# Buffers of raw weights in the MLPs of a two-layer diffusion block: two pools in turn, or each pool by the number of its buffers

## The chip, the cores and the metric

The kernel runs as one program on one core of one Trainium2 chip. The metric is device time in microseconds, as the median of several runs. One further run is recorded by the hardware profiler, and the profile's numbers come from that one. Engines are named as the profile names them: PE is TensorE's matmuls and PEld its weight loads, DVE is VectorE, ACT is ScalarE, POOL is GpSimd. SP is the engine that issues most transfers; its queue is worked off in order.

## The reference

The block has a latent stream of 256 tokens and a context of 256 tokens, with 2048 channels in float32. Two layers follow each other. The first mixes tokens with a bidirectional RWKV-7 recurrence, the second with a gated long convolution (Hyena). After each mixer comes a dense MLP with a squared ReLU, 2048 to 8192 channels and back. Each part stands between two RMS norms, with shift, scale and gate computed from a conditioning vector (adaLN):

```
h = modulate(rms_norm(x, norm_g[i, 2]), mod[:, 3], mod[:, 4])
x = x + mod[:, 5] * rms_norm(squared_relu_mlp(h, mlp_up[i], mlp_down[i]), norm_g[i, 3])
```

Here `squared_relu_mlp(h, w_up, w_down)` is `square(relu(h @ w_up)) @ w_down`, and `mod` is `silu(c) @ ada_w[i] + ada_b[i]`, a product of one row with a matrix of 2048 by 12288 per layer. The weights of one MLP take 128 MB in float32, and each is used once.

## The kernel before

**Products in three terms.** A float32 operand is split into a high part, which ScalarE rounds to the format that TensorE multiplies, and a low part, the rest, which VectorE subtracts (`split_into`). `mm3` then multiplies high by high, high by low and low by high into one accumulator in PSUM. All large products are made so.

**Weights.** `load_split` (L139) brings one block of weights: it takes a raw tile `w` of 128 by 2048 float32 (1 MB), issues its transfer on SP, and splits it in halves of 1024 columns into tiles `wh` and `wl`, the cast on ScalarE and the subtraction on VectorE. A raw tile is free again when its last half has been split. A split half is free when the last matmul that reads it has been done.

**Pools.** `open_weights` (L86) opens a pool of raw tiles (`wraw`) and a pool of split halves (`wsp`) and puts each into a list. From layer 0's output projection to the end one pair is open, with two raw tiles and three halves of each part. Inside `mlp` (L1489) a second pair is opened beside it, `MLPW = (1, 3)`: one raw tile and three halves. So an MLP has three raw tiles and six halves; the products around it have two and three. `turn` (L94) moves the last pool of a list to its front and takes the tile from it. With one pool in the list it always gives that pool; within a pool the tiles go round.

**The MLP.** `mlp` runs in four parts of 2048 hidden channels. Each part first makes the up product (`gemm_ws`, L176): the weights stand in TensorE, and 258 columns stream through (256 tokens and two columns for the shift). A load of 1 MB gives 48 such matmuls. Eight blocks of 256 channels take two loads each. The first part begins with a lead (`lead`): its first two blocks are made side by side from eight loads of 512 KB, so that the first matmuls need only the first channels of the normalised input `hx`, which `resid` (L433) of the part before makes one block of channels after the other. The results are evacuated to `nt`, squared, and split into `uh` and `ul`. Then the down product (`gemm_tok`, L211) adds 16 loads of 1 MB into eight accumulators, two at a time, with 24 matmuls of 512 columns to a load. There are 132 loads in an MLP.

**Beside it.** During the MLPs a generator, `ada_run` (L304), computes the adaLN rows that later layers need. It loads tiles `aw` of 512 KB on the same SP queue (two buffers) and accumulates them into `acc`, on VectorE for the rows computed in the first MLP, on ScalarE and GpSimd for later ones. `tick` advances it after each weight load, at a rate that spreads it over the MLP.

**Order.** The order of the instructions on each engine is made once, when the program is built: a planner goes through the instructions by priority (mostly program order), gives out tiles of the pools, and when an instruction has to wait for a tile, a later one of the same queue can be placed ahead of it. On the chip each engine works its list in order.

Of the kernel before, what the change touches and what calls it, by code (L numbers as in the profile page):

```python
# [69 lines left out]
class Kern:  # L70
# [15 lines left out]
    def open_weights(self, es, raw=2, sp=3):  # L86

        for l, n, b in ((self.wraw, "wraw", raw), (self.wsp, "wsp", sp)):
            if b:
                l.append(self.pool(es, n, b))  # L90
                es.callback(l.pop)

    @staticmethod
    def turn(pools):  # L94
# [1792 lines left out]
```

## Time and profile before

| what | value |
|---|---|
| runs | 3564.54, 3571.8 and 3573.12 us, median 3571.8 us |
| the profiled execution's own time | 3562.79 us |
| its span | 3561.0 us |
| granted TensorE clock, mean | 0.974 |
| PE busy | 3312.7 us, 93% of the span |
| DVE, ACT, POOL busy | 2450.2, 1738.5 and 435.3 us |
| moved from and to HBM | 777.31 MB read, 54.59 MB written |
| first MLP, issues of its weights after the product before it | 1456.8 to 2227.0 us |
| second MLP, the same | 2772.1 to 3512.6 us |

The span runs from the first to the last instruction of the program. A group of instructions is given with its source line; most operations of the two engines ACT and DVE go through one helper (L53) and all large matmuls through another (L111), so the groups are told apart by the names of the tiles: `wh<-w` is a cast of raw weights, `wl<-w,wh` a subtraction, `mm<-wh,uh` a matmul of the down product, `mm<-hxh,wh` one of the up product, `acc<-aw,sc,acc` a step of the adaLN rows. "Idle before" is the time that an engine stood still just before an instruction, with what ended it. The chain of waits follows the work that ended last back to what released it.

### The profile page before, as it was taken

How to read it: one execution, taken by the hardware profiler on the slowest of the kernel's cores; microseconds unless marked ns; L12 is line 12 of the kernel's file. 1: busy time of each engine (PE TensorE's matmuls, PEld its weight loads, DVE VectorE, ACT ScalarE, POOL GpSimd, SP SyncE). 2: the span in 40 equal slices, each digit the busy share in tenths (PEclk: the TensorE clock that was granted, in tenths of full speed). 3: DMA queues.
4: the chain of work that ended last, by engine and by line, in shares of the span. 5: the costliest groups of instructions: out<-in, count | busy, mean ns of one | idle time of the engine just before them, and what ended most of it. 6: DMA issues, size and time to landing. Idle time of an engine off the chain costs nothing.

```text
span 3561.0 us, 74541 instructions
## 1 busy us (share of the span) xinstructions
PE 3312.7 (93%) x30598; PEld 2890.3 (81%) x30598; DVE 2450.2 (69%) x3867; ACT 1738.5 (49%) x3070; POOL 435.3 (12%) x496
## 2 busy tenths in 40 slices
PE   6798888999999798999999999999999899999999
PEld 3476677878888666898979898898887798989897
DVE  4788776767777765687777776688786675555554
ACT  4554454545544454443434345566564664434343
POOL 0011121111111000000000002134441530000000
PEclk9999999999999899999999999999999999999999
DMA  9668898999988646678888887566665775565563
GB/s 309 208 221 291 270 344 265 286 277 274 274 273 272 195 131 209 206 255 288 266 287 267 291 256 242 166 222 220 218 213 189 235 240 186 188 185 182 189 187 122
DMA packets 587808, 836.79 MB, mean 235 GB/s; under 512 B 39552, under 2 KB 373281, under 8 KB 587465
## 3 DMA queue, kind: packets, MB, share of 16 engines
q1 hardware_dynamic: 556360, 718.76, 62.9%
q0 software_dynamic: 31104, 113.26, 10.0%
q8 instruction: 239, 3.92, 0.4%
q14 instruction: 105, 0.85, 0.1%
HBM read 777.31 MB, written 54.59 MB: 234 GB/s over the span
## 4 chain that ended last, share of the span: by engine, by line
PE 54%; DMA 19%; DVE 14%; ACT 6%; issue 5%; POOL 2%; SPq 0%; ACTq 0%; DVEq 0%; POOLq 0%
PE mm L111 39%; DMA aw<-in_ada_w 10%; PE fl L111 5%; PE sg L111 5%; PE sc L111 4%; DVE wl L53 3%; POOL acc L329 2%; DVE acc L53 1%; DVE tmp L53 1%; DVE d L53 1%; ACT aw L53 1%; ACT wh L53 1%; DMA w<-in_mlp_down 1%; DVE xt L53 1%; DMA cum<-cum 1%
## 5 line engine op out<-in xcount | busy, mean ns | idle before, releaser
L53 DVE TENSOR_TENSOR wl<-w,wh 128x1024 fp32r<-128x1024 f32 (+1 forms) x716 | 912.5, 1280 | 514.6 <-ACT wh L53 511.2
L53 ACT CAST wh<-w 128x1024 fp32r<-128x1024 f32 (+1 forms) x716 | 737.8, 1043 | 694.0 <-PE mm L111 390.3
L111 PE MATMUL mm<-hxh,wh 128*128 128x258 f32 x2816 | 803.4, 286 | 13.0 <-DVE nt L53 11.6
L111 PE MATMUL mm<-hxh,wl 128*128 128x258 f32 x2816 | 801.4, 285 | 4.6 <-DVE wl L53 4.5
L111 PE MATMUL mm<-hxl,wh 128*128 128x258 f32 x2816 | 799.3, 284 | 0.0
L111 PEld LDWEIGHTS mm<-hxh,wh 128*128 128x128 f32 x2816 | 534.1, 190 | 16.9 <-DVE nt L53 9.0
L111 PEld LDWEIGHTS mm<-hxh,wl 128*128 128x128 f32 x2816 | 534.2, 190 | 8.2 <-DVE wl L53 6.8
L111 PEld LDWEIGHTS mm<-hxl,wh 128*128 128x128 f32 x2816 | 536.7, 191 | 1.8
L329 POOL TENSOR_TENSOR acc<-acc,aw 128x512 f32<-128x512 f32 x180 | 274.6, 1526 | 1341.4 <-ACT aw L53 1239.9
L111 PE MATMUL mm<-wh,uh 128*128 128x512 f32 x1024 | 405.5, 396 | 0.7 <-DVE nt L53 0.7
L111 PE MATMUL mm<-wl,uh 128*128 128x512 f32 x1024 | 400.7, 391 | 1.9 <-DVE wl L53 1.8
L111 PE MATMUL mm<-wh,ul 128*128 128x512 f32 x1024 | 402.4, 393 | 0.0
L53 DVE SCALAR_TENSOR_TENSOR acc<-aw,sc,acc 128x512 f32<-128x512 f32 x300 | 225.0, 750 | 102.7 <-DMA aw<-in_ada_w 100.5
L111 PEld LDWEIGHTS mm<-wl,uh 128*128 128x128 f32 x1024 | 192.4, 188 | 48.6 <-DVE wl L53 5.7
L111 PEld LDWEIGHTS mm<-wh,ul 128*128 128x128 f32 x1024 | 192.2, 188 | 45.6
L111 PE MATMUL fl<-fh,fx 128*128 128x256 f32 x1024 | 214.8, 297 | 13.2 <-DMA fx<-xv 11.2
L111 PEld LDWEIGHTS mm<-wh,uh 128*128 128x128 f32 x1024 | 192.3, 188 | 41.9 <-DVE nt L53 1.1
L111 PEld LDWEIGHTS fl<-fh,fx 128*128 128x128 f32 x1024 | 168.7, 194 | 31.5 <-DMA fx<-xv 14.6
L53 ACT ACTIVATE aw<-aw,sc 128x512 f32<-128x512 f32 x180 | 125.8, 719 | 131.0 <-DMA aw<-in_ada_w 128.0
L111 PE MATMUL fl<-flo,fx 128*128 128x256 f32 x512 | 146.0, 285 | 0.0
L111 PE MATMUL sg<-ard,KB 64*64 64x64 f32 (+1 forms) x3584 | 128.6, 244 | 13.9 <-ACT yf L53 4.5
L111 PEld LDWEIGHTS sg<-ard,KB 64*64 64x64 f32 x3584 | 110.0, 136 | 20.1 <-ACT yf L53 4.7
(361 smaller groups left out, 5867.5 us busy)
## 6 DMA issues: line engine op xcount, KB each, us to landing
aw<-in_ada_w SPq DMA_DIRECT2D x288, 512.0 KB, 6.0
w<-in_mlp_down SPq DMA_DIRECT2D x128, 1024.0 KB, 5.4
w<-in_mlp_up SPq DMA_DIRECT2D x120, 1024.0 KB, 6.6
fx<-xv POOLq DMA_DIRECT2D x128, 512.0 KB, 6.1
aw<-in_ada_w SPq DMA_DIRECT2D x192, 256.0 KB, 3.8
w<-in_hy_in_w SPq DMA_DIRECT2D x44, 1024.0 KB, 5.3
fx<-xr POOLq DMA_DIRECT2D x64, 512.0 KB, 5.7
w<-in_w_k SPq DMA_DIRECT2D x16, 1024.0 KB, 7.5
```

What stands on the lines that cost most here:

```text
L53: return self.kern.pin(self.key, f(*a, **kw))
L111: return self.pin("pe", self.nc.tensor.matmul(out, lhsT=lhsT, rhs=rhs, **kw))
L329: nc.gpsimd.tensor_tensor(acc, acc, w[:, a], op=ALU.add)
```

## The change

The list of pools gets each pool as often as the pool has buffers, where it had each pool once. `turn` is unchanged and still moves the last entry to the front. When the pools of an MLP are closed, every entry of that pool is taken out of the list, where before the last entry was popped.

```
         for l, n, b in ((self.wraw, "wraw", raw), (self.wsp, "wsp", sp)):
             if b:
-                l.append(self.pool(es, n, b))
-                es.callback(l.pop)
+                p = self.pool(es, n, b)
+                l.extend([p] * b)
+                es.callback(lambda l=l, p=p: l.__setitem__(slice(None), [q for q in l if q is not p]))
```

In an MLP the list of raw tiles was outer, own and is now outer, outer, own. From its start the raw tiles were taken own, outer, own, outer, and are now taken own, outer, outer, own, outer, outer. The list of split halves was outer, own and is now three times outer and three times own; halves were taken from the two pools in turn and are now taken three from the own pool, then three from the outer. Outside the MLPs a list holds one pool only, once or several times, and the tiles are taken as before. The number and size of the buffers, the loads and all computation are the same.

## The prediction

> **What bounds the kernel now.** I read the page first, then the busy times of stretches inside the two MLPs, then in the worst stretch the matmul groups, the chain of waits and the tile of raw weights.
>
> ```profile
> PE 3312.7 (93%) x30598; PEld 2890.3 (81%) x30598; DVE 2450.2 (69%) x3867; ACT 1738.5 (49%) x3070; POOL 435.3 (12%) x496
> GB/s 309 208 221 291 270 344 265 286 277 274 274 273 272 195 131 209 206 255 288 266 287 267 291 256 242 166 222 220 218 213 189 235 240 186 188 185 182 189 187 122
> w<-in_mlp_up SPq DMA_DIRECT2D x16, 512.0 KB, 5.3
> ```
>
> TensorE is busy 93% of the span. The change can give back only time in which TensorE stands in an MLP because raw weights are late. So I count matmuls. The columns are stretch, length, then busy time and count for PE, PEld, DVE, ACT and POOL, granted clock, DMA share and GB/s.
>
> ```profile
> 1530.00:1770.00 240.00, 240.00 (x1649) 223.61 (x1648) 183.97 (x260) 102.85 (x155) 0.00 (x0) 1.00 0.84 273
> 1770.00:1920.00 150.00, 143.64 (x824) 123.99 (x823) 110.86 (x145) 54.45 (x73) 0.00 (x0) 1.00 0.85 281
> ...
> 2070.00:2120.00 50.00, 47.83 (x392) 46.91 (x391) 35.75 (x52) 20.56 (x33) 0.00 (x0) 1.00 0.82 260
> ...
> 2900.00:3530.00 630.00, 630.00 (x3878) 566.57 (x3878) 350.27 (x418) 282.69 (x395) 2.31 (x2) 1.00 0.58 185
> 3100.00:3160.00 60.00, 60.00 (x262) 48.83 (x261) 29.61 (x29) 23.09 (x22) 0.00 (x0) 1.00 0.59 191
> 3020.00:3080.00 60.00, 60.00 (x501) 60.00 (x500) 36.20 (x51) 30.06 (x51) 0.00 (x0) 1.00 0.58 183
> ```
>
> The last two rows are pure stretches of the second MLP: a matmul of the down product takes 60/262 = 0.229 us, one of the up product 60/501 = 0.120 us. One load of 1 MB feeds 24 of the first or 48 of the second, so TensorE uses one up in 5.50 or 5.75 us.
>
> ```profile
> L111 PE MATMUL mm<-wl,uh 128*128 128x512 f32 x128 | 50.8, 397 | 1.9 <-DVE wl L53 1.8
> L111 PE MATMUL mm<-hxh,wh 128*128 128x258 f32 x136 | 39.0, 287 | 3.7 <-DVE nt L53 3.7
> L312 PE MATMUL sg<-ones,acc 128*128 128x2 f32 x32 | 3.8, 241 | 0.0
> ```
>
> Each product has three matmul groups of the same count, so 1770 to 1920 us holds 384 down, 408 up and 32 small ones (0.12 us each, like an up one): 87.9 + 48.9 + 3.8 = 140.6 us of work in 150, **9.4 us lost**. From 2070 to 2120 the 392 matmuls, nearly all up, need 47.0 of 50: **3.0 us lost**. From 1530 to 1770 and from 2900 to 3530 TensorE is never idle. So 12.4 us is what the steady parts can return, all in the first MLP.
>
> Who makes it wait, in 1770 to 1920 us, by the chain of waits and by the tile of raw weights:
>
> ```profile
> by line: DMA w<-in_mlp_down 20.2%; DMA aw<-in_ada_w 15.4%; DVE wl L53 15.3%; PE mm L111 13.3%; DVE acc L53 11.6%; DMA w<-in_mlp_up 9.2%; issue 7.3%; ACT wh L53 4.2%; DVE o L53 2.0%; DVE nt L53 0.7%; PE sg L312 0.5%; DVE mod L53 0.1%; ACTq L
> ...
> 1778.93 7.99 DMA w<-in_mlp_down
> 1786.99 1.06 ACT wh L53
> ...
> 1792.12 7.83 DMA w<-in_mlp_down
> ```
> ```profile
> L53 DVE TENSOR_TENSOR wl<-w,wh x49: 1212/1217/1225, 1770.2 to 1916.8; 128x1024 fp32r<-128x1024 f32 x49
> L53 ACT CAST wh<-w x49: 1027/1046/1054, 1770.7 to 1919.6; 128x1024 fp32r<-128x1024 f32 x49
> L53 SPq DMA_DIRECT2D w<-in_mlp_down x14: 367/368/368, 1771.4 to 1849.4; - x14
> L53 SPq DMA_DIRECT2D w<-in_mlp_up x11: 367/368/368, 1855.4 to 1918.0; - x11
> its engine sat idle before it (us, times) until:
>   DMA w<-in_mlp_down: 38.4, 7
>   DMA w<-in_mlp_up: 33.7, 5
> ...
> DMA to landing us min/median/max: 7.2/7.6/8.1
> ```
>
> The chain is a ring: a load is issued at 1778.93, lands 7.99 us later, its cast starts within 0.1 us, two casts and two subtractions follow, and the subtraction's end lets the next load go at 1792.12. A turn takes 13.19 us. ScalarE waits 72.1 us for 12 of these 25 loads: every second one is late.
>
> **The change part by part.** In the code before, load n of an MLP takes its slot by parity. Even loads share the one slot of the MLP's own pool, so load n waits for the split of load n−2; odd ones have the outer pool's two slots and wait for n−4. The ring above is the single slot's: one turn per two loads, 13.19/2 = 6.6 us per load, against the 5.50 us that TensorE needs. After the change the list holds the outer pool twice and the own pool once, so every load waits for the split of n−3: one turn per three loads, 13.19/3 = **4.4 us per load**, below 5.50. The k-th load on SP still goes when a third-last split ends, now in program order, so bytes and queue places stay nearly as they are. Nothing is added: the same loads, casts and subtractions.
>
> *Split halves.* The six halves before came one from each pool in turn; now three from one, then three from the other. Either way a half comes back after six: 0 us. The order would matter only with unequal pools.
>
> *The steady gain.* The raw-weight ring goes. The other ring in this stretch, the adaLN weights, stays:
>
> ```profile
> L53 DVE SCALAR_TENSOR_TENSOR acc<-aw,sc,acc x57: 739/747/754, 1773.4 to 1915.8; 128x512 f32<-128x512 f32 x57
> L53 SPq DMA_DIRECT2D aw<-in_ada_w x31: 367/368/368, 1770.0 to 1916.5; - x31
> ...
> DMA to landing us min/median/max: 3.8/5.3/7.5
> ```
> ```profile
> by line: PE mm L111 44.0%; DMA aw<-in_ada_w 13.4%; DMA w<-in_mlp_up 11.7%; DVE wl L53 11.0%; DVE acc L53 6.7%; issue 5.8%; DVE nt L53 2.2%; ACT wh L53 2.1%; PE sg L312 1.6%; DVE o L53 1.4%; DVE mod L53 0.1%; ACTq L53 0.1%; DVEq L53 0.1%
> ```
>
> Its turn is 0.37 + 5.3 + 2 × 0.75 = 7.2 us over two buffers, 3.6 us per load; with 31 of them beside 25 weight loads that is 4.5 us per 5.50, but at the longest landing (7.5 us) 5.8, which is too slow. So it is late only at times. By the chain's shares the weights' part of the loss is 29.4/44.8 of 9.4 us, 6.2, and (second row, 2070 to 2120) 11.7/25.1 of 3.0 us, 1.4: together 7.6. That leaves 4.8 us in which the adaLN load was last. Part of that is late only because VectorE and SP, both in order, stood behind a late split. Bounds: 0 (that ring takes the place at once) and 12.4. I take 7.6 plus half of 4.8, **−10.0 us**.
>
> *Second MLP, steady (2900 to 3530 us).* Nothing: the casts wait for TensorE, and loads land sooner.
>
> ```profile
>   PE mm L111: 284.2, 185
> ...
> DMA to landing us min/median/max: 5.0/5.3/7.4
> ```
>
> *The entries.* The MLP's own slot is also what lets its first loads run ahead while the product before is still working:
>
> ```profile
> 1372.31 0.59 SPq L53 DMA_DIRECT2D w<-in_mlp_up  x1
> ...
> 1380.76 0.37 SPq L53 DMA_DIRECT2D w<-in_mlp_up  x1
> ...
> 1386.82 0.69 SPq L53 DMA_DIRECT2D w<-in_mlp_up  x1
> ...
> 1399.73 0.37 SPq L53 DMA_DIRECT2D w<-in_mlp_up  x1
> ```
> ```profile
> 1390.00:1410.00 20.00, 17.70 (x77) 14.04 (x76) 8.56 (x9) 8.20 (x8) 0.00 (x0) 1.00 0.87 291
> ...
> 2820.00:2900.00 80.00, 76.68 (x622) 75.74 (x621) 59.45 (x67) 54.06 (x96) 44.67 (x29) 0.99 0.76 241
> ```
> TensorE's waits, from 1457 to 2290 us and from 2737 to 3561:
> ```profile
> PE mm L111 <- DVE nt L53: 10.0, 6, 4.1
> PE sg L459 <- DVE dg L53: 7.6, 2, 4.2
> ```
> ```profile
> PE sg L459 <- DVE dg L53: 12.2, 2, 9.6
> PE mm L111 <- DVE nt L53: 2.4, 2, 2.1
> ```
>
> The four issues ahead of the first MLP are its loads 0, 2, 4 and 6 of 512 KB, each issued when the slot's last split ended. After the change the slot holds loads 0 and 3, and load 3's split needs a half of the outer pool, so it stands until the earlier product lets one go. Two early loads and two early splits per entry move behind the product. In the first entry they leave a crowded moment (0 to 1.8 us of gain, 512 KB at 291 GB/s) and find gaps later, since TensorE then waits for the norm anyway (`dg`): 0. In the second entry ScalarE is busy 54 of 80 us with adaLN weights too: 0 to 2 × (1.05 + 1.22) = 4.5 us. The longest wait for the norm there, 9.6 us, covers most; I take a quarter, **+1.1**. After an MLP the outer pool's halves come free up to two halves later; without the same wait for `dg` at the MLP's end that would cost a half's matmuls, 2.8 us, with it 0.
>
> The sum is −10.0 + 1.1 = **−8.9 us**. The profiled execution took 3562.79 us (span 3561.0), so its like would take 3553.9. It is 9.0 us below the median of the runs, 3571.8, and near the fastest, 3564.54. On the median's footing the forecast is **3562.9 us**.
>
> **The rivals.**
>
> *The adaLN ring takes over.* If its loads are always the last, the weights come early for nothing: 0 to −3, time about 3570. For it: its landing of up to 7.5 us, and 15.4% of the chain. Against it: 4.5 us per load at the median. The Trainium skill, DMA: Bandwidth & Descriptors, section Issuing engines are not separate DMA queues, says that all DMAs run on the same 16 engines and interleave, by which a weight load sent earlier could only delay an adaLN load and the gain would be nil; but the number of loads in flight rises little, and the stretch moves 281 GB/s where one slice of the page moves 344, so the trace leaves it room.
>
> *More goes than the steady loss.* TensorE also waits early in each MLP for the up product's evacuation (`nt`, longest 4.1 us and 2.4 in all). If ScalarE, freed of its waits, serves these sooner, the whole 12.4 goes and 4.1 + 2.4 with it: −18.9, time 3552.9. Against it: the rows name VectorE, whose work the change leaves as it is.
>
> *Slower: the lost head start.* In the lead part TensorE consumes eight small loads. If loads 4 and 5, and then 7 and 8, each have to wait for a turn of the outer slots (0.37 + 5.3 landing + 1.05 + 1.22 = 7.9 us), each entry loses 15.9 us and both 31.8; less 10.0 that is +21.8, time **3593.6**. It decides once the two entries lose over 10 us together. For it: in the entry to the second MLP both DMA and ScalarE are loaded. Against it: the lead part is paced by the residual's columns, which come one after another, and loads 1 and 2 now have free halves waiting.
>
> *It does not do what it says.* Were the slots given out without regard to the turn, nothing would change. The pairing seen above (every second load late) speaks against that; it is in the first rival's time.
>
> **How the numbers follow.** Forecast 0.50, adaLN ring or no effect 0.18, more than the steady loss 0.20, slower 0.12. A measurement of this kernel can tell about 0.3% (10.7 us) from no change. Faster by more: all of the third case and 0.18 of the forecast's, 0.38. Slower: 0.11 of the last. Same: 0.51. The range reaches from the larger gain (3552.9, less 3 for runs as fast as the fastest) to 3575, the adaLN case with the highest run's 1.3 us and some of the entry cost; it leaves out most of the slower case.
>
> **What would show it.** Right: in the first MLP ScalarE's wait for raw weights falls from 72.1 us in the like of 1770 to 1920 to under 20; in the chain the weights' share falls below that of the adaLN load; TensorE's busy time there is near full; and ahead of the MLPs SP shows two small loads instead of four. Wrong: those waits stay; or they go while VectorE's wait for adaLN weights rises by as much; or TensorE idles in the lead parts.

## The result and the profile after

The changed kernel took **3555.46 us** (median of 8 runs, 3544.67 to 3563.14) beside 3573.61 us for the kernel before (8 runs, 3564.54 to 3580.38). The ratio is 0.9937, with a 95% interval of 0.9921 to 0.9954: 0.63% faster. The forecast was 8.9 us less than before; the medians differ by 18.2 us. Direction and main mechanism were right; the forecast had half of the size.

The two profiled executions show less than that. Here is the head of the page after:

```profile
span 3558.3 us, 74568 instructions
...
PE 3310.4 (93%) x30598; PEld 2894.7 (81%) x30598; DVE 2453.0 (69%) x3867; ACT 1749.9 (49%) x3070; POOL 436.7 (12%) x496
```

The span fell from 3561.0 to 3558.3 us, 2.7 us. So the spans can't be compared as they stand. Up to the output projection of layer 0 the two programs have the same instructions on every engine, yet that part took 1375.4 us in the profile before and 1389.6 us in this one; over all the profiles of this case it took 1370 to 1400 us. The table cuts that scatter off. Its stages are read from TensorE's instructions: from the first matmul of the output projection to the first down matmul of the first MLP ("entry 1"), from there to the last down matmul of that MLP ("MLP 1"), to the first down matmul of the second MLP ("entry 2", with the residual and Hyena), and to the last down matmul ("MLP 2"). An end of some 18 us follows. "Before, again" and "after, again" are one more profiled execution of each.

| kernel (us) | entry 1 | MLP 1 | entry 2 | MLP 2 | sum |
|---|---|---|---|---|---|
| before | 217.0 | 657.1 | 660.7 | 632.9 | 2167.7 |
| before, again | 218.7 | 658.5 | 662.3 | 632.9 | 2172.4 |
| after | 219.7 | 641.0 | 661.5 | 629.4 | 2151.6 |
| after, again | 220.4 | 641.0 | 659.5 | 629.4 | 2150.3 |

From the means, MLP 1 gives 16.8 us, MLP 2 gives 3.5, entry 1 costs 2.2 and entry 2 gives 1.0: 19.1 us, about what the runs show. Within a stage of an MLP the same kernel repeats to 1.4 us or better; an entry repeats to about 2 us, so what the entries cost or give is hardly told from nothing.

**Where the time went in MLP 1.** The busy time of the same stretches as before, after the change (stretch, length, PE, PEld, DVE, ACT, POOL, granted clock, DMA share, GB/s):

```profile
1770.00:1920.00 150.00, 150.00 (x907) 134.27 (x906) 117.82 (x157) 63.73 (x84) 0.00 (x0) 1.00 0.87 292
1920.00:2070.00 150.00, 150.00 (x906) 134.25 (x906) 119.28 (x163) 64.90 (x88) 0.00 (x0) 1.00 0.88 293
2070.00:2120.00 50.00, 50.00 (x421) 50.00 (x419) 41.94 (x63) 24.96 (x41) 0.00 (x0) 1.00 0.87 273
```

TensorE, which worked 143.64 of the first 150 us and 47.83 of the last 50, now works all of them. The chain of waits by line, for 1770 to 1920 us and for 2070 to 2120 us:

```profile
by line: PE mm L112 98.0%; PE sg L313 2.1%
...
by line: PE mm L112 97.1%; PE sg L313 3.1%
```

No transfer is left in it: neither the raw weights (29.4% before in the first stretch) nor the adaLN weights (15.4%). The tile of raw weights in 1770 to 1920 us (line numbers after are one higher):

```profile
L53 ACT CAST wh<-w x53: 1032/1049/1057, 1769.9 to 1919.0; 128x1024 fp32r<-128x1024 f32 x53
L53 DVE TENSOR_TENSOR wl<-w,wh x51: 1214/1218/1228, 1771.3 to 1918.5; 128x1024 fp32r<-128x1024 f32 x51
L53 SPq DMA_DIRECT2D w<-in_mlp_down x15: 367/368/368, 1772.6 to 1853.0; - x15
L53 SPq DMA_DIRECT2D w<-in_mlp_up x11: 367/368/368, 1859.1 to 1919.8; - x11
its engine sat idle before it (us, times) until:
  PE mm L112: 60.1, 36
...
DMA to landing us min/median/max: 5.8/6.7/7.4
```

ScalarE's 72.1 us of waits for raw weights are gone from this stretch. It waits 60.1 us for TensorE instead, that is, for a split half to come free: the weights now run ahead of the matmuls. Over the whole MLP, 1500 to 2250 us, the waits (us in total, times, longest) were before

```profile
ACT wh L53 <- DMA w<-in_mlp_down: 113.1, 23, 11.3
ACT wh L53 <- DMA w<-in_mlp_up: 111.4, 23, 11.2
...
ACT wh L53 <- PE mm L111: 48.4, 30, 4.5
...
DVE acc L53 <- DMA aw<-in_ada_w: 78.9, 44, 5.0
```

and are after

```profile
ACT wh L53 <- PE mm L112: 228.6, 151, 4.0
...
DVE acc L53 <- DMA aw<-in_ada_w: 78.5, 50, 3.7
...
ACT wh L53 <- DMA w<-in_mlp_down: 5.9, 3, 2.3
```

46 late loads of weights became 3. VectorE's wait for adaLN weights stayed what it was.

**MLP 2.** There was no stall to remove there, and still it is 3.5 us shorter. The rows that answer to those shown of before:

```profile
2900.00:3530.00 630.00, 629.51 (x3901) 568.26 (x3900) 352.78 (x423) 284.24 (x397) 2.72 (x2) 1.00 0.58 186
...
3100.00:3160.00 60.00, 60.00 (x264) 49.20 (x263) 30.10 (x29) 23.10 (x22) 0.00 (x0) 1.00 0.56 189
```

TensorE is full in both kernels but for 0.5 us, and in 60 us it makes 264 matmuls where it made 262. The distance from the start of one down matmul to the start of the next, the spacing, went from 230.7 to 229.0 ns in this MLP; over its 1536 down matmuls that is 2.7 us. That of its 2304 up matmuls went from 120.3 to 119.9 ns, 0.9 us. The prediction had no term for either.

### The profile page after: what moved, and what is told of

It reads as the page before. It is cut to its first block, busy times and chain, and to the rows that moved or that the text cites. A ratio compares the mean times of both kernels' runs of the same rounds, so it can differ in the third digit from the quotient of the medians.

```text
span 3558.3 us, 74568 instructions
## 1 busy us (share of the span) xinstructions
PE 3310.4 (93%) x30598; PEld 2894.7 (81%) x30598; DVE 2453.0 (69%) x3867; ACT 1749.9 (49%) x3070; POOL 436.7 (12%) x496
## 4 chain that ended last, share of the span: by engine, by line
PE 60%; DMA 16%; DVE 11%; ACT 5%; issue 4%; POOL 2%; SPq 1%; ACTq 0%; DVEq 0%; POOLq 0%
PE mm L112 45%; DMA aw<-in_ada_w 9%; PE sg L112 5%; PE fl L112 5%; PE sc L112 4%; POOL acc L330 2%; DVE tmp L53 1%; DVE wl L53 1%; DVE d L53 1%; ACT aw L53 1%; ACT wh L53 1%; DMA win<-in_window 1%; PE sc L414 1%; DMA cum<-cum 1%; PE sg L460 1%
## 5 line engine op out<-in xcount | busy, mean ns | idle before, releaser
L53 ACT CAST wh<-w 128x1024 fp32r<-128x1024 f32 (+1 forms) x716 | 745.8, 1044 | 642.6 <-PE mm L112 578.7
```

What stands on the lines that cost most here:

```text
L53: return self.kern.pin(self.key, f(*a, **kw))
```

## Experiments

All are compared with runs of the kernel before on the same chip. Stage times are from one profile each; they are put together in a table at the end.

**The two kernels again,** the changed one in six runs and the kernel before in one, to see what repeats.

> The changed kernel a second time, beside the kernels of this group. By every theory -18 us against the kernel before (between -12 and -24). Its profile is a second sample: if the parts before layer 0's output projection, whose instructions are the same in both kernels, take another time than in the first sample, then a part of the difference between two single profiles is scatter of the recurrence, and the stages have to be compared one by one.

> The kernel before a second time, one look: its stages in a second sample. From the first down product of the first MLP to its last, 657 us as in the first sample if the late weights are a property of the program (within 1.5 us), and the mean distance of two down matmuls in the second MLP 0.2307 us; the recurrence ahead of it may differ by 10 us and more.

Measured: the changed kernel 3551.71 us (6 runs) beside 3569.93, ratio 0.9942 [0.9924, 0.9959], again 18.2 us between the medians. The kernel before took 3570.31 us in its one run beside 3572.91. Their stages are in the table above.

**The two edits apart: raw tiles alone.** Only the raw tiles' pool is put into the list as often as it has buffers.

```
-                p = self.pool(es, n, b)
-                l.extend([p] * b)
+                p = self.pool(es, n, b)
+                l.extend([p] * (b if n == "wraw" else 1))
```

> The list of raw tiles as in the change, the list of split halves as before (one from each pool in turn). Raw-slot theory (each load now waits for the split of the third last, not every second one for the second last): the whole effect, -18 us, between -13 and -24; ScalarE's wait for raw weights in the first MLP falls as in the changed kernel. Halves theory (the matmuls of the MLPs run 0.5 to 1% faster because three halves in turn lie in one pool): only -10, and the mean distance of two matmuls of the down product in the second MLP stays at 0.231 us.

Measured: 3558.04 us (12 runs) beside 3569.93, ratio 0.9968 [0.9953, 0.9983]. ScalarE's waits in 1500 to 2250 us, and two stretches:

```profile
ACT wh L53 <- PE mm L111: 226.8, 147, 4.5
...
ACT wh L53 <- DMA w<-in_mlp_down: 11.4, 4, 3.6
```
```profile
1770.00:1920.00 150.00, 150.00 (x900) 133.57 (x899) 116.67 (x155) 63.27 (x83) 0.00 (x0) 1.00 0.89 292
...
3100.00:3160.00 60.00, 60.00 (x261) 48.80 (x260) 30.53 (x28) 22.62 (x22) 0.00 (x0) 1.00 0.57 186
```

The waits go and TensorE is full in MLP 1, which takes 644.3 us, 12.8 less than before. MLP 2 stays at 632.9 us, at the old count of 261 in 60 us. The gaps between TensorE's matmuls beyond their usual spacing, taken from their starts, add up to 14.2 us in MLP 1 of the kernel before and to 1.3 us here. So the order of the raw tiles removes the stalls, nearly all of them, and leaves the spacing as it was. Neither theory of the expectation holds alone: the runs gave 11.9 us, less than the 13 to 24 of the raw-slot theory, and the spacing stayed, as the halves theory said.

**The split halves alone.** The same edit with `"wsp"` in place of `"wraw"`.

> The list of split halves as in the change (three from one pool, then three from the other), the list of raw tiles as before. Raw-slot theory: about 0, between -4 and +4; every second raw load late as before. Halves theory: -8 us, from 3072 matmuls of the down products at 2 to 3 ns less, with their mean distance in the second MLP at 0.229 instead of 0.231 us.

Measured: 3566.04 us (12 runs) beside 3569.93, ratio 0.9985 [0.9967, 1.0003]; by the runs alone this is not told from nothing. The profile is clearer. ScalarE's waits in 1500 to 2250 us and the same two stretches:

```profile
ACT wh L53 <- DMA w<-in_mlp_down: 110.0, 23, 10.5
ACT wh L53 <- DMA w<-in_mlp_up: 108.2, 26, 11.4
```
```profile
1770.00:1920.00 150.00, 143.74 (x815) 124.23 (x814) 112.30 (x149) 56.75 (x77) 0.00 (x0) 0.99 0.84 277
...
3100.00:3160.00 60.00, 60.00 (x264) 49.23 (x263) 29.48 (x28) 23.26 (x23) 0.00 (x0) 1.00 0.56 189
```

All stalls of before are there, and the closer spacing of MLP 2 is there too (264 in 60 us; MLP 2 629.4 us). MLP 1 takes 655.0 us, 2.1 less than before. The spacing belongs to the halves alone, though it is worth less than the 8 us of the expectation's halves theory: the two MLPs together give 5.6 us.

**The ring by its number of slots.** If the ring is what cost the time, the MLP without a raw tile of its own should be no better than before, and a fourth tile should add nothing to three taken by number. Both are the kernel before with one number changed, so the list is still taken in turn.

```
-    MLPW = (1, 3)
+    MLPW = (0, 3)
```

> The kernel before, but the MLPs open no raw tile of their own: two raw tiles for all loads, each of which waits for the split of the second last; halves as before. Raw-slot theory, in which one slot serving every second load set the pace before and the third tile was worth little: one turn of 13.2 us per two loads as before, so 0 to +20 us. If instead the third tile was of use before, then now both slots are late in turn in the first MLP and the 132 loads lose 1.1 us each where TensorE needs 5.5: some +60 us or more.

Measured: 3590.36 us (6 runs) beside 3569.93, ratio 1.0052 [1.0034, 1.0070]. ScalarE's waits in 1500 to 2250 us:

```profile
ACT wh L53 <- DMA w<-in_mlp_up: 142.8, 49, 8.3
ACT wh L53 <- DMA w<-in_mlp_down: 135.3, 41, 7.2
```

That is 20.4 us more, just past the end of the raw-slot theory's range and far from the other's 60. There are 90 late loads where before had 46. The turn of the ring per load is the same as before (load n waits for n−2, where before every second one did), but now most loads are late, with none in time between them to make up for it: MLP 1 takes 672.4 us, 15.3 more. The third tile was thus worth 15 us even when it was taken at the wrong time, and 13 more when it was taken in the right order.

```
-    MLPW = (1, 3)
+    MLPW = (2, 3)
```

> The kernel before with one more raw tile in the MLP's own pool, pools taken in turn as before, so that every load waits for the split of the fourth last; halves as before. Raw-slot theory: as the kernel that has only the raw tiles by number, -12 us (-8 to -17), with the first MLP at 643 to 645 us and no gain over the third last, because 4.4 us per load is already below the 5.5 that TensorE needs. If the adaLN loads or the DMA engines are what limits then: the same or less. If even three slots still cost something: a first MLP under 641 us.

Measured: 3563.34 us (12 runs) beside 3572.91, ratio 0.9972 [0.9955, 0.9990]. The tile of raw weights in 1770 to 1920 us:

```profile
its engine sat idle before it (us, times) until:
  PE mm L111: 56.5, 34
...
DMA to landing us min/median/max: 7.2/7.3/9.4
```

MLP 1 takes 644.3 us, the same as three tiles in the right order. Waiting for the third-last split is enough; a fourth 1 MB tile buys no further time.

**The kernel after with halves that never change pool.** To see whether stepping from one pool of halves to the other is what spaces the matmuls, the MLP gets four halves of its own and leaves the outer three unused.

```
+            outer = [q for q in self.wsp if q is not self.wsp[-1]]
+            self.wsp[:] = [q for q in self.wsp if q is self.wsp[-1]]
+            es.callback(lambda: self.wsp.__setitem__(slice(0, 0), outer))
...
-    MLPW = (1, 3)
+    MLPW = (1, 4)
```

> The changed kernel, but in the MLPs the split halves come from the own pool alone, which has four of them (the outer pool's three stand idle there): a ring of four in one place, never a step from one pool to the other. If each step between the pools costs matmul time (the difference of 0.2307, 0.2290 and, in the output projection with one pool, 0.2267 us): 0.2267 us in the second MLP, 3 to 4 us less there. If the spacing of the halves in time or their number does it: 0.229 or more. In the first MLP fewer halves ahead of TensorE may bring back idle time: 0 to +12 us. In all -5 to -18 us against the kernel before.

Measured: 3554.08 us (6 runs) beside 3572.91, ratio 0.9946 [0.9926, 0.9965]. The pure down stretch of MLP 2:

```profile
3100.00:3160.00 60.00, 60.00 (x267) 49.67 (x266) 30.71 (x29) 23.11 (x22) 0.00 (x0) 1.00 0.57 194
```

267 in 60 us: the spacing is 226.8 ns, and MLP 2 takes 626.7 us, 2.7 less again. MLP 1 takes 641.7 us, about what it took with six halves, but here two things cancel: the spacing of its down matmuls fell from 228.8 to 227.0 ns, 2.8 us in all, and the gaps beyond the spacing rose from 1.3 to 4.5 us. With four halves TensorE has to wait a little again. The gain over the changed kernel is too small for the runs to show.

**Seven halves, four own and three outer, by number.**

```
-    MLPW = (1, 3)
+    MLPW = (1, 4)
```

> The changed kernel with four halves in the MLP's own pool beside the outer pool's three, by number: four in turn from one, three from the other. If steps between pools cost: two steps in seven halves instead of two in six, 0.2287 us or a little less; raw theory: no idle time in the first MLP is left that a seventh half could take. So the same as the changed kernel, -18 us against the kernel before (-12 to -24).

Measured: 3554.7 us (6 runs) beside 3572.91, ratio 0.9943 [0.9924, 0.9962]; MLP 2 628.9 us. Neither better nor worse than the changed kernel.

**The same kernels at another place in SBUF.** The spacing, sorted by the half that the matmuls read, depends on which half came before. In ns, mean distance of the down matmuls of MLP 2, from their starts (a step is a half of another pool than the half before):

| kernel | first own half (step) | next own | first outer (step) | next outer |
|---|---|---|---|---|
| before (each half is a step) | 230.8 to 231.0 | – | 230.3 | – |
| after | 230.8 | 226.7, 227.1 | 230.3 | 229.4, 228.9 |

Either the step costs in itself (some 4 ns into the own pool, 1 into the outer), or the place of the tiles does. Both kernels were built once more with the MLP's own weight pools opened ahead of its other pools. By the addresses in the built programs the own halves then begin 45 KB behind the outer ones in each partition, where it was 100 KB, and the split activations `ul`, `uh`, which lay between, lie behind both.

```
-            mp, mu = self.pool(es, "mp"), self.pool(es, "mu", 16)
             self.open_weights(es, *self.MLPW)
+            mp, mu = self.pool(es, "mp"), self.pool(es, "mu", 16)
```

> The changed kernel with the MLP's own pools opened ahead of the pools of its activations, so that in each partition of SBUF the own halves begin 45 KB behind the outer ones where it was 100 KB, and the activations u (ul, uh) lie behind both, 23 to 80 KB from the own halves (before: 0 to 65 KB) and 68 to 125 KB from the outer ones (before: 35 to 92 KB). The same loads and matmuls. The place also overlaps the activations of the output projection, so that the own pools can't be filled ahead of the first MLP: its lead part may lose up to 16 us by the lost head start of the prediction, or nothing. In question is the time from one matmul of the second MLP's down product to the next, 230.8 ns in the first own half after an outer one, 226.9 in the next own ones, 230.3 in the first outer one, 229.2 in the next outer ones, 229.0 on the mean. Theory A, the distance between successive halves costs: the step halves fall by about half of their 4 ns to 228 or 229, the others stay or fall, the mean is 228.0 or less. Theory B, every step from pool to pool costs whatever the distance: the step halves stay at 230 to 231 and the mean at 229. Theory C, the distance from a half to u costs: the own halves rise to 229 and the outer ones to 230 or 231, the mean is 229.5 or more. The time follows the spacing by 768 matmuls a part and six parts, 4.6 us per ns in all, and the lead.

> The kernel before with the same change of place: own and outer halves taken in turn, each half a step from pool to pool, at 45 KB where it was 100 KB. The mean distance of the second MLP's down matmuls before is 230.7 ns. Theory A (distance between successive halves): 229 or less. Theory B (every step costs the same): 230.7. Theory C (distance to u): 230.7 or more.

Measured, on the kernel after: 3549.63 us (4 runs) beside 3576.01, ratio 0.9922 [0.9893, 0.9952]; its interval overlaps the changed kernel's, so it isn't shown to be better. On the kernel before: 3583.5 us (10 runs), ratio 1.0027 [1.0009, 1.0045].

| kernel | first own half (step) | next own | first outer (step) | next outer |
|---|---|---|---|---|
| after, new place | 228.9 | 228.9, 229.0 | 228.9 | 229.4, 228.9 |
| before, new place (each half is a step) | 229.0 | – | 228.9 to 229.4 | – |

A pure down stretch of the kernel before at the new place:

```profile
3130.00:3190.00 60.00, 60.00 (x263) 49.23 (x263) 29.44 (x28) 23.03 (x23) 0.00 (x0) 1.00 0.57 188
```

Theory B falls: with the same order, each half a step, the spacing is 228.9 to 229.4 ns at one place and 230.3 to 231.0 ns at the other, and MLP 2 takes 628.7 us in both kernels of the new place. But neither of the others holds whole. A said that halves that are no step would stay or fall; the own ones rose from 227 to 229, as C said. C said that the outer ones would rise; they stayed. So the spacing depends on where the MLP's tiles lie in SBUF, and the rule of it stays open. (The 4.6 us per ns of the first expectation is too much for the down matmuls: both MLPs have 3072 of them, so a nanosecond of their spacing is worth 3.1 us.)

This pair shows one thing more. At the new place the own tiles overlap the output projection's activations, so nothing can be loaded ahead of the first MLP: SP issues its first weight 11 us before the projection's last matmul, where the kernel before issued four loads from 95 us ahead of it on. TensorE's waits from 1457 to 1560 us (in total, times, longest), kernel before at the new place:

```profile
PE mm L111 <- ACT wh L53: 7.5, 4, 5.6
PE sg L459 <- DVE dg L53: 4.1, 1, 4.1
```

and kernel after at the new place:

```profile
PE sg L460 <- DVE dg L53: 2.6, 1, 2.6
...
PE mm L112 <- ACT wh L53: 0.4, 2, 0.2
```

Taken in turn, the tiles let TensorE wait 7.5 us for weights in the lead; taken by number, 0.4 us with no load ahead at all. The table puts the other stages beside.

| kernel (us) | entry 1 | MLP 1 | entry 2 | MLP 2 |
|---|---|---|---|---|
| raw tiles by number alone | 217.4 | 644.3 | 665.3 | 632.9 |
| halves by number alone | 219.0 | 655.0 | 659.7 | 629.4 |
| before, two raw tiles | 225.0 | 672.4 | 661.1 | 632.9 |
| before, four raw tiles | 220.3 | 644.3 | 663.3 | 632.9 |
| after, four own halves only | 220.2 | 641.7 | 667.5 | 626.7 |
| after, seven halves | 220.4 | 640.6 | 663.6 | 628.9 |
| after, new place | 213.3 | 640.6 | 661.3 | 628.7 |
| before, new place | 224.5 | 664.7 | 672.9 | 628.7 |

The kernel before at the new place also takes 6.9 us longer in MLP 1, 6.7 in entry 1 and 11.4 in entry 2 (over the means of before), and 4.2 us less in MLP 2. In MLP 1 it is more of the same stall: ScalarE waits 265.8 us for 54 late weight loads in 1500 to 2250 us, where before it waited 224.5 us for 46. Why more are late, and what lengthens entry 2, isn't shown. The profiled execution was the slowest of its ten, 9 us above their median, so these stages overstate what the runs lost (7.5 us).

## Why the prediction was right, and where it was not

**The bound and the ring: right.** The prediction read 12.4 us of stalls in the first MLP's steady parts from counts of matmuls, and named the single slot's ring. Raw tiles by number alone took 12.8 us out of MLP 1 (657.1 to 644.3) and left no idle time in those stretches. What the prediction asked for as a sign came: waits for raw weights under 20 us (none listed in 1770 to 1920), no share of them in the chain, TensorE full. Four slots giving the same 644.3 us shows that waiting for the third-last split is early enough.

**"I take 7.6 plus half of 4.8, −10.0": mis-sized, the whole 12.4 went.** The prediction took 4.8 us as the part in which an adaLN load came last, and let half of it remain. Nothing remained. The adaLN ring is as late as before: VectorE's wait for it is 78.9 us before, 78.5 after and 78.1 with the raw tiles alone. But it no longer reaches TensorE, because the splits now run ahead by as much as the halves allow (ScalarE waits 228.6 us for TensorE, where it waited 48.4). A share of the chain told which wait was last, not which would still matter with a cushion in front of it.

**"The adaLN ring takes over": wrong, by the same numbers.** The prediction cited the Trainium skill (DMA: Bandwidth & Descriptors, section Issuing engines are not separate DMA queues) for all transfers running on the same 16 engines and interleaving, and inferred for this rival that weight loads sent earlier could only delay the adaLN loads. The inference is the prediction's; the section doesn't state it. Here the stretch went from 281 to 292 GB/s, and the adaLN loads of it landed no later at the median:

```profile
L53 SPq DMA_DIRECT2D aw<-in_ada_w x32: 367/368/792, 1773.6 to 1918.3; - x32
...
DMA to landing us min/median/max: 3.7/4.8/8.1
```

The median is 4.8 us for 5.3 before, the longest 8.1 for 7.5. The trace doesn't bear the inference out: earlier weight loads had no price in TensorE's time here.

**"Split halves: 0 us": the step that failed.** The prediction reasoned that a half comes back after six either way, and so costed the order at nothing. As far as waiting goes that is right. But the order also sets which addresses TensorE reads in turn, and that changed the spacing of the matmuls: 3.5 us in MLP 2 (632.9 to 629.4, with the halves alone as with both edits) and 2.1 to 3.3 us in MLP 1 (halves alone against before; both edits against raw tiles alone). That is about 6 us of the 18. For the same reason "second MLP, steady: nothing" was off by 3.5 us.

**The entries: about right in sum, small either way.** The prediction had 0 and +1.1 us. The stage table has +2.2 and −1.0 us from two profiles each, and their scatter of about 2 us leaves both unproven. Of the four early loads of each entry two went, as it said; SP's issues ahead of the first MLP are now

```profile
1386.50 0.60 SPq L53 DMA_DIRECT2D w<-in_mlp_up  x1
...
1394.98 0.37 SPq L53 DMA_DIRECT2D w<-in_mlp_up  x1
```

The price that it saw in the second entry is there too, if small. TensorE's waits from 2737 to 3561 us, after, hold a wait for split weights that before didn't have:

```profile
PE mm L112 <- DVE wl L53: 4.0, 4, 1.6
```

Its waits for `nt` in the same stretch fell from 2.4 to 0.5 us, and the entry as a whole got no longer.

**"Slower: the lost head start": refuted.** It needed over 10 us lost in the two entries. The changed kernel lost 1.2 us in both together. At the new place, with no early load in the first entry, the kernel after took 213.3 us there, less than any other, and 661.3 us in the second. Of the two kernels at the new place, the one with the new order waited 0.4 us for weights there, the one with the old order 7.5 us.

**"More than the steady loss": the nearest time (3552.9), half of its cause.** That rival said that the whole 12.4 us would go, which they did, and 4.1 + 2.4 us of waits for `nt` in the lead parts with them. TensorE's waits in the first MLP and what leads to it, 1457 to 2290 us, are after

```profile
PE sg L460 <- DVE dg L53: 11.8, 2, 8.5
...
PE mm L112 <- DVE nt L53: 2.1, 1, 2.1
```

where before had 10.0 us for `nt` and 7.6 for `dg`. But of those 10.0 us, 5.9 (five waits of at most 1.5 us) fell between 1779 and 2102 us, in the stretches with late weights, and so belong to the 12.4. In the lead, 1457 to 1560 us, the waits were before

```profile
PE sg L459 <- DVE dg L53: 4.2, 1, 4.2
PE mm L111 <- DVE nt L53: 4.1, 1, 4.1
```

and after

```profile
PE sg L460 <- DVE dg L53: 8.5, 1, 8.5
...
PE mm L112 <- DVE nt L53: 2.1, 1, 2.1
```

The lead only waits for another thing, and entry 1 as a whole didn't get shorter. The gain beyond the steady loss came from the spacing. The prediction's range reached down to 3549.9 us for this rival's sake; that 3555.46 lies in it is in part luck, since some 6 us came by a way that no part of the prediction had.

By its own terms, then: −12.8 for −10.0, about −6 for 0, about +1 for +1.1. That makes −18, the difference of the medians.

## What to carry to other kernels

Where buffers come from unequal pools, count for each slot how many loads come to it: taking pools in turn gave one of three slots half of the loads, and cost 13 us that the right order gave back without another buffer. When you cost the removal of a late transfer, ask what else is late behind a cushion that will now exist; a second ring that was late on its own engine cost nothing here, because it no longer reached the bound. And a single profile can hide or feign a gain: compare the stages that the change touches, not the spans, when a part that it doesn't touch scatters by more than the effect.

## What the runs showed of the hardware

**Matmul spacing depends on where the tiles lie.** The same instruction, 128 by 128 on 128 by 512, followed the one before at 226.8, 229 or 230.7 ns on the mean, with TensorE always busy, a granted clock of 1.00 and the same instructions around it. Within the groups of three that make one product, the spread is regular: at 229 the three are spaced 232, 226 and 229 ns, at 226.8 all are spaced 226 to 228. What differs is the place of raw tiles, halves and activations in SBUF, and in one place also whether the half before lay 100 KB away. The work of ScalarE and VectorE beside it is not the cause: down matmuls of the second MLP that started while neither worked kept their distances, 230.8 ns before, 229.1 after and 226.7 with four own halves (49 to 83 of them each). What the transfers write meanwhile wasn't varied. Distance between halves alone, distance to the activations alone and a fixed price for each step between pools each fail on at least one of the rows above. Which addresses matter, and how, is open; over an MLP it is worth 2 to 6 us.

**One part scatters on its own.** The part up to the output projection, with the same instructions on every engine in before and after, took between 1370.2 and 1389.6 us in their four profiles, while an MLP repeats to 1.4 us or better. What makes it scatter wasn't tried.
